# Heads' k, v and q products in pools of their own, gates through DRAM, two sets of projection banks, and first splits in another order

## The chip, the cores and the metric

The kernel runs on one core of a Trainium2 chip. The time is device microseconds of one execution. TensorE (PE) multiplies matrices into PSUM, VectorE (DVE) and ScalarE (ACT) work on tiles between PSUM and SBUF, GpSimd (POOL) helps them, and SyncE (SP) issues most of the DMAs. Each engine runs its own instructions in order, and waits on semaphores for those of the others.

## The reference, cut to what matters

Layer 0 is a gated pooling mixer, layer 1 a multi-head latent attention with 16 heads; SEQ is 512, D_MODEL 2048, W_A 4096, the latents have 512 channels.

```python
def pool_mixer_layer(x, norm_g, w_in, w_group, scale, w_out):
    h = rmsnorm(x, norm_g)
    proj = h @ w_in
    u, gate = proj[..., :W_A], proj[..., W_A:]
    pooled = jnp.stack([causal_mean_pool(u[:, :, gi], w) - u[:, :, gi] for gi, w in enumerate(POOL_WINDOWS)], axis=2)
    y = jnp.einsum('bsgc,gcd->bsgd', pooled, w_group).reshape(B, S, W_A) * scale
    y = y * jax.nn.silu(gate)
    return x + y @ w_out

def shared_kv(...):
    c = rmsnorm(c, kv_latent_g)
    kv = (c @ kv_w_b).reshape(B, S, N_HEADS, QK_NOPE + V_HEAD)
    k = qk_norm_rope(jnp.concatenate([k_nope, k_rope], axis=-1), k_norm_g, cos, sin)

def mla_layer(x, k, v, norm_g, w_in, q_latent_g, w_q_b, q_norm_g, w_out, cos, sin):
    proj = h @ w_in
    q_lat, gate = proj[..., :Q_LORA], proj[..., Q_LORA:]
    q = (rmsnorm(q_lat, q_latent_g) @ w_q_b).reshape(B, S, N_HEADS, QK_HEAD)
    q = qk_norm_rope(q, q_norm_g, cos, sin)
    o = chunk_causal_attention(q, k, v).reshape(B, S, W_B)
    return x + (o * jax.nn.silu(gate)) @ w_out
```

## The kernel before

Every product of float32 numbers is made of three matmuls: an operand is split into a high part, rounded by ACT (`A.copy`), and a low part, the rest, by DVE (`V.tensor_tensor(lo, src, f(hi), subtract)`; this helper, `split`, is at L147 to L149). PE then multiplies high by high, high by low and low by high. `load_w` (L115 to L127) fetches a tile of weights, raw, and splits it into `whi` (L125, ACT) and `wlo` (L126, DVE); `proj` with `mm3` (L143 to L145) multiplies it into one of three `mm` banks.

**Stage 1** is the first product, h @ w_in. Four output tiles are made by plain products (L357 to L382, 8 rounds of j): in each round two x tiles are loaded (`x_load`, L272 and L273), four weight tiles (L366), x is split with its gain (`gsplit`, L152 to L154), the weights are split in two halves of two tiles each, and PE runs L379 to L381. Round 0 is issued with high priority. The remaining 60 tiles are made in 30 pairs with seven products instead of eight (`w_combos`, `seven` with L328, L330, L332, and `gather`, L334 to L351, which puts the results together in a tile `e` and stores it in DRAM as `scr`). A pair takes four PSUM banks, k0 to k3, from a pool `ps7` with two buffers of each.

**Stage 2** takes the 4 groups of 8 tiles: `pooled_tile` (L428 on) loads a tile from `scr`, pools it and splits it into two `at` tiles; the eight of group 0 need no pooling any more and are issued with high priority. `y_tile` (L438 on) multiplies them by w_group (awg) and the gate; w_out (awo) follows. During group 0 the 16 x tiles are loaded again (xT, L458). The banks of stage 2 (`ps`: mm, sc, tr, ov) take the place of `ps7`.

**Attention.** `gate_unit` (L577 on) makes the 16 gates, silu of a projection, and keeps them in `at` tiles. Eight head groups of two heads follow. For the next group `prep_units` makes k and v (`kv_unit`, L613 to L615), q (`q_unit`, L633 to L635), the rotation of q on POOL (`qrot_unit`, L681 to L684) and the transposes (`tr_unit`; its u == 5 splits the rotary part of q in two halves, L714 on ACT and L715 on DVE). Beside it runs the attention of the present group: `score_unit` (scores L739, maximum L742, exp L747, scaling L748 and L749), two steps later `pt_unit` (transposes L758, split) and after each second one `pv_unit` (probabilities times v, L783 to L785; after the second of a head the product with the gate, L788). Two lists, one of attention and one of the preparation, are merged by due times (`LEAD`, `PACE`), and the tile framework's scheduler then sets each engine's order by the data and by when the pools' buffers come free. Last, `og_unit` splits the gated outputs and `out_unit` multiplies them by w_out (bwo); the first of these run beside the last group.

Pools: `xpool` (tiles `xt`, 16 buffers) holds raw k and q, v of group 0 and the split probabilities; `bpool` (`bt`, 32) holds transposed k and q and the later groups' v; `apool` (`at`, 32) holds latents and gates; the pool of `tt_` (7 in attention) holds probabilities, the rotary parts and other short-lived tiles. `tr` has two banks.

## Time and profile before

| | us |
|---|---|
| three runs | 1950.3, 1948.01, 1948.62 |
| profiled execution, its own time | 1948.62 |
| its span in the profile | 1946.8 |
| PE busy | 1920.0 (99%) |
| DVE, ACT, POOL busy | 1277.0, 822.7, 258.7 |
| DMA | 235.53 MB, mean 121 GB/s |

The busy time of PE counts a matmul from its start to its modelled end, so that neighbours overlap; how fast PE goes is read from start to start. In rows of single instructions the columns are the start, the duration, the engine and line, the operation and the tiles, and in square brackets how long the engine was idle before it and what released it. In tables by stretch each engine has its busy time and, in brackets, its instructions; then come the granted clock of TensorE, the DMA share and GB/s.

### The profile page before, as it was taken

The page shows a single profiled execution, that of the slowest core. Times are in us where ns is not written, and L with a number is a line of the kernel's source. Part 1 is how long each engine was busy: PE and PEld are TensorE (multiplying, and loading weights), DVE is VectorE, ACT ScalarE, POOL GpSimd, SP SyncE. Part 2 cuts the span into 40 slices and gives each one's busy share as a digit, 9 for nine tenths or more (in the row PEclk, how much of TensorE's full clock was granted, in tenths as well). Part 3 has the DMA queues.
Part 4 walks back from the last instruction along what each step waited for, and adds up shares of the span by engine and source line. Part 5 has one row for each costly group of instructions (what it writes and reads, how often), then busy time and mean ns, then how long its engine had stood idle before and what let it go on. Part 6 is the DMA issues. An engine that isn't in the chain of part 4 may idle for free.

```text
span 1946.8 us, 30577 instructions
## 1 busy us (share of the span) xinstructions
PE 1920.0 (99%) x11356; PEld 1707.5 (88%) x11356; DVE 1277.0 (66%) x2297; ACT 822.7 (42%) x1570; POOL 258.7 (13%) x405
## 2 busy tenths in 40 slices
PE   8999999999999999999999999999999999999999
PEld 7999999999999878888888888888888888888887
DVE  8677786896666687485685567473344888796432
ACT  7443433333333433333333454232244777785221
POOL 0433333344223000000000000000010111110000
PEclk9999999999999999999999999999999999999999
DMA  6545444445444655344334343333332111121632
GB/s 194 161 151 161 152 131 130 127 130 168 132 130 136 195 163 156 114 125 141 115 127 139 114 146 122 90 93 101 97 92 72 56 39 54 47 69 50 216 119 87
DMA packets 167894, 235.53 MB, mean 121 GB/s; under 512 B 14656, under 2 KB 94912, under 8 KB 167744
## 3 DMA queue, kind: packets, MB, share of 16 engines
q1 hardware_dynamic: 167568, 233.37, 38.4%
q8 instruction: 89, 1.46, 0.3%
q14 instruction: 61, 0.50, 0.1%
q10 hardware_dynamic: 144, 0.20, 0.0%
q0 software_dynamic: 32, 0.00, 0.0%
HBM read 208.35 MB, written 25.17 MB: 120 GB/s over the span
## 4 chain that ended last, share of the span: by engine, by line
PE 87%; DVE 5%; DMA 4%; ACT 3%; issue 1%; SPq 0%; POOL 0%; DVEq 0%; ACTq 0%; POOLq 0%
PE mm L145 14%; PE mm L143 14%; PE mm L144 14%; PE k L332 10%; PE k L328 9%; PE k L330 9%; PE sc L739 2%; PE mm L613 2%; PE mm L614 1%; PE mm L615 1%; PE mm L633 1%; PE mm L634 1%; PE k L379 1%; PE mm L635 1%; PE k L380 1%
## 5 line engine op out<-in xcount | busy, mean ns | idle before, releaser
L125 ACT CAST whi<-raw 128x512 fp32r<-128x512 f32 (+2 forms) x421 | 252.9, 608 | 515.6 <-PE mm L144 443.8
L328 PE MATMUL k<-xc,hi 128*128 128x256 f32 x1680 | 460.2, 283 | 0.0
L330 PE MATMUL k<-xc,hi 128*128 128x256 f32 x1680 | 460.2, 283 | 0.0
L126 DVE TENSOR_TENSOR wlo<-raw,whi 128x512 fp32r<-128x512 f32 (+2 forms) x421 | 281.1, 671 | 238.2 <-ACT whi L125 234.5
L332 PE MATMUL k<-xc,lo 128*128 128x256 f32 x1680 | 418.0, 284 | 0.4 <-DVE lo L312 0.2
L311 ACT CAST hi<-raw 128x1792 fp32r<-128x1792 f32 x120 | 202.8, 1690 | 359.6 <-PE k L332 240.6
L312 DVE TENSOR_TENSOR lo<-raw,hi 128x1792 fp32r<-128x1792 f32 x120 | 248.9, 2074 | 153.2 <-ACT hi L311 153.1
L145 PE MATMUL mm<-bt,wlo 128*128 128x512 f32 x860 | 336.0, 391 | 0.6 <-DVE wlo L126 0.6
L143 PE MATMUL mm<-bt,whi 128*128 128x512 f32 x860 | 335.1, 390 | 1.1 <-ACT bt L148 1.1
L144 PE MATMUL mm<-bt,whi 128*128 128x512 f32 x860 | 334.6, 389 | 0.0
L330 PEld LDWEIGHTS k<-xc,hi 128*128 128x128 f32 x1680 | 322.7, 192 | 0.0
L328 PEld LDWEIGHTS k<-xc,hi 128*128 128x128 f32 x1680 | 322.7, 192 | 0.0
L332 PEld LDWEIGHTS k<-xc,lo 128*128 128x128 f32 x1680 | 296.9, 192 | 1.5 <-DVE lo L312 1.0
L143 PE MATMUL mm<-at,whi 128*128 128x512 f32 x516 | 201.0, 391 | 1.9 <-DVE e L339 1.3
L144 PE MATMUL mm<-at,whi 128*128 128x512 f32 x516 | 201.9, 391 | 0.4 <-DVE at L149 0.4
L145 PE MATMUL mm<-at,wlo 128*128 128x512 f32 x516 | 201.4, 390 | 0.9 <-DVE wlo L126 0.9
L145 PEld LDWEIGHTS mm<-bt,wlo 128*128 128x128 f32 x860 | 161.5, 188 | 35.9 <-DVE wlo L126 2.2
L143 PEld LDWEIGHTS mm<-bt,whi 128*128 128x128 f32 x860 | 161.5, 188 | 35.3 <-ACT bt L148 1.6
L144 PEld LDWEIGHTS mm<-bt,whi 128*128 128x128 f32 x860 | 161.5, 188 | 33.6 <-DVE bt L149 0.2
L307 POOL TENSOR_TENSOR raw<-raw 128x256 f32<-128x256 f32 x120 | 99.9, 833 | 429.8 <-DVE raw L305 405.9
L143 PEld LDWEIGHTS mm<-at,whi 128*128 128x128 f32 x516 | 96.7, 188 | 22.6 <-DVE e L339 1.5
L145 PEld LDWEIGHTS mm<-at,wlo 128*128 128x128 f32 x516 | 96.9, 188 | 22.3 <-DVE wlo L126 2.3
(1150 smaller groups left out, 2589.1 us busy)
## 6 DMA issues: line engine op xcount, KB each, us to landing
raw<-awin SPq DMA_DIRECT2D x240, 256.0 KB, 3.3
raw<-awo SPq DMA_DIRECT2D x128, 256.0 KB, 2.8
raw<-bwin SPq DMA_DIRECT2D x80, 256.0 KB, 2.7
raw<-awg SPq DMA_DIRECT2D x64, 256.0 KB, 2.8
raw<-bwo SPq DMA_DIRECT2D x59, 256.0 KB, 2.8
scr<-e SPq DMA_DIRECT2D x56, 256.0 KB, 2.6
raw<-wkvb SPq DMA_DIRECT2D x32, 256.0 KB, 2.9
raw<-wqb SPq DMA_DIRECT2D x32, 192.0 KB, 2.4
```

Of the source, the lines that this page charges most:

```text
L125: A.copy(hi[:, :n], raw[:, :n])
L126: V.tensor_tensor(lo[:, :n], raw[:, :n], f(hi[:, :n]), ALU.subtract)
L143: T.matmul(dst, wh, xh, start=first, stop=False)
L144: T.matmul(dst, wh, xl, start=False, stop=False)
L145: T.matmul(dst, wl, xh, start=False, stop=last)
L307: G.tensor_tensor(c[:, :, 6, :], c[:, :, 4, :], c[:, :, 2, :], ALU.add)
L311: A.copy(hi, c[:, :, 1:8, :])
L312: V.tensor_tensor(lo, c[:, :, 1:8, :], f(hi), ALU.subtract)
L328: T.matmul(dst, hi[:, j % 2, wi, :], xh[j][:, xi, :], start=first, stop=False, skip_group_check=True)
L330: T.matmul(dst, hi[:, j % 2, wi, :], xl[j][:, xi, :], start=False, stop=False, skip_group_check=True)
L332: T.matmul(dst, lo[:, j % 2, wi, :], xh[j][:, xi, :], start=False, stop=last, skip_group_check=True)
L613: T.matmul(acc, ch[:, tsl], hi, start=(k == 0), stop=False)
```

## The change

Five things change. (1) In round j of the plain products the second x tile and the second half of the weights are loaded later, and the first half of the weights is split before the second x part; the rounds' x pools stand in another order; the load of `post` moves from POOL's queue to ACT's. (2) `ps7` becomes two pools with one buffer of each bank; the plain products take the second set, and pair n the set n % 2. (3) The first `y_tile` is issued only after the fourth split of group 0's pooled tiles. (4) Gates are stored in DRAM (`gd`), fetched into a `bt` tile at the third score of their head, multiplied there, and, but for the last head group, the gated output is stored in the same place and fetched again by `og_unit` into a `tt_` tile. (5) Raw k and v move to `at`, raw q to a new pool `qpool` of 5 buffers, for which `xpool` shrinks from 16 to 11; k's rotary part goes to `bt` from group 1 on.

```diff
@@ -77,8 +77,11 @@
-    def at(dt=F32R):
-        return apool.tile([P, S], dt, tag="a", name="at")
+    def qt(shape=(P, S)):
+        return qpool.tile(list(shape), F32, tag="q", name="qt")
+
+    def at(dt=F32R, shape=(P, S)):
+        return apool.tile(list(shape), dt, tag="a", name="at")
@@ -145,8 +148,7 @@
     def split(src, hi, lo):
-        A.copy(hi, src)
-        V.tensor_tensor(lo, src, f(hi), ALU.subtract)
+        return A.copy(hi, src), V.tensor_tensor(lo, src, f(hi), ALU.subtract)
@@ -174,7 +176,7 @@
     post = const.tile([P, 4], I32, name="post")
-    nc.gpsimd.dma_start(post, pos)
+    nc.scalar.dma_start(post, pos)
     tabs = {}
@@ -261,20 +263,22 @@
-        xcp = {j: c1.enter_context(tc.tile_pool(name=f"xcp{j}", bufs=1, **tile_)) for j in (3, 2, 6, 5, 4, 1, 0, 7)}
+        xcp = {j: c1.enter_context(tc.tile_pool(name=f"xcp{j}", bufs=1, **tile_)) for j in (4, 2, 6, 5, 3, 1, 0, 7)}
         w7 = c1.enter_context(tc.tile_pool(name="w7", bufs=2, **tile_))
-        ps7 = c1.enter_context(tc.tile_pool(name="ps7", bufs=2, space=bass.MemoryType.PSUM))
+
+        ps7 = [c1.enter_context(tc.tile_pool(name=f"ps7{i}", bufs=1, space=bass.MemoryType.PSUM, **tile_))
+               for i in range(2)]
         xh, xl = [None] * NJ, [None] * NJ
...
             nc.sync.dma_start(c[:, 2:8:5, :], xT[2 * j].rearrange("p (h t) -> p h t", h=2))
+            return c
+
+        def x_parts(j, c, hp):
+
             nc.sync.dma_start(c[:, 0:2, :], xT[2 * j + 1].rearrange("p (h t) -> p h t", h=2))
-            return c
-
-        def x_parts(j, c, hp):
-
             hl = xcp[j].tile([P, 2, 7, H], F32R, tag="xc", name="xc")
@@ -312,8 +316,8 @@
-        def banks():
-            return [ps7.tile([P, 2, H], F32, tag=f"k{i}", name=f"k{i}") for i in range(4)]
+        def banks(n):
+            return [ps7[n % 2].tile([P, 2, H], F32, tag=f"k{i}", name=f"k{i}") for i in range(4)]
@@ -351,7 +355,7 @@
-        accs = [ps7.tile([P, 2, H], F32, tag=f"k{i}", name=f"k{i}") for i in range(4)]
+        accs = banks(1)
         with ExitStack() as c2:
@@ -362,12 +366,14 @@
                 lo = w7.tile([P, 4, 2, P], F32R, tag="lo", name="lo")
-                for o in range(4):
-                    nc.sync.dma_start(
-                        raw[:, o, :, :], awin[32 + o][:, 2 * j * P:2 * (j + 1) * P].rearrange("p (k n) -> p k n", k=2))
-                h12, l12 = x_parts(j, c, hp)
-                for o in (0, 2):
-                    split(raw[:, o:o + 2], hi[:, o:o + 2], lo[:, o:o + 2])
+                parts = None
+                for m in (0, 2):
+                    for o in (m, m + 1):
+                        nc.sync.dma_start(raw[:, o, :, :], awin[32 + o][:, 2 * j * P:2 * (j + 1) * P].rearrange(
+                            "p (k n) -> p k n", k=2))
+                    parts = parts or x_parts(j, c, hp)
+                    split(raw[:, m:m + 2], hi[:, m:m + 2], lo[:, m:m + 2])
+                h12, l12 = parts
                 c4.close()
@@ -403,7 +409,7 @@
         for n, pair in enumerate((*range(18, 32), *range(16))):
-            ks = banks()
+            ks = banks(n)
             for q in range(NJ // 2):
@@ -412,14 +418,15 @@
                 V.tensor_tensor(sq[0], sq[0], sq[1], ALU.add)
-                p = ps7.tile([P, 2, H], F32, tag="k3", name="k3").rearrange("p h t -> p (h t)")
+                p = ps7[0].tile([P, 2, H], F32, tag="k3", name="k3").rearrange("p h t -> p (h t)")
                 ra[0] = norm_r(sq[0], D, p)
...
     bpool = ctx.enter_context(tc.tile_pool(name="bpool", bufs=32, **tile_))
-    xpool = ctx.enter_context(tc.tile_pool(name="xpool", bufs=16, **tile_))
+    xpool = ctx.enter_context(tc.tile_pool(name="xpool", bufs=11, **tile_))
+    qpool = ctx.enter_context(tc.tile_pool(name="qpool", bufs=5, **tile_))
     tp[0] = ca.enter_context(tc.tile_pool(name="tpool2", bufs=6, **tile_))
@@ -432,7 +439,7 @@
         hi, lo = at(), at()
-        split(x, hi, lo)
+        splits.append(split(x, hi, lo))
         return hi, lo
@@ -447,14 +454,22 @@
+    splits = []
     with tc.high_priority():
...
     for g in range(NG):
-        ys = [y_tile(g, o, pooled) for o in range(8)]
+        ys = []
+        for o in range(8):
+            with ExitStack() as c5:
+                if g == 0 and o == 0:
+
+                    for ins in splits[3]:
+                        c5.enter_context(tc.issue_after(ins.ins))
+                ys.append(y_tile(g, o, pooled))
         if g == 0:
...
             for k in range(KD):
-                x = xt()
+                x = xt() if k < 11 else qt()
                 nc.sync.dma_start(x, xT[k])
@@ -578,15 +593,17 @@
         V.tensor_tensor(z, acc, rb[0], ALU.mult)
-        sg = at(F32)
-        A.activation(sg, z, AF.Silu)
-        gates.append(sg)
+        A.activation(z, z, AF.Silu)
+        gd = dpool.tile([P, S], F32, tag="gd", name="gd")
+        nc.sync.dma_start(gd, z)
+        gates.append(gd)
...
     SC = 192.0 ** -0.5
-    st = {}
+    st, gated = {}, {}
+    nhg = NH // 2
@@ -594,11 +611,12 @@
         d["kvw"] = [load_w(wkvb[hg, :, k * 512:(k + 1) * 512], 512) for k in range(4)]
-        d["kraw"] = [xt((P, 2, 256)) for _ in range(2)]
+
+
+        d["kraw"] = [at(F32, (P, 2, 256)) for _ in range(2)]
         d["qraw"] = [None] * 4
-        vt = bt if hg else xt
-        d["vh"] = [vt((P, 2, 256), F32R) for _ in range(2)]
-        d["vl"] = [vt((P, 2, 256), F32R) for _ in range(2)]
+        d["vh"] = [at(F32R, (P, 2, 256)) for _ in range(2)]
+        d["vl"] = [at(F32R, (P, 2, 256)) for _ in range(2)]
         d["ssk"] = small(8, "ssk", 2)
@@ -633,7 +651,7 @@
             T.matmul(acc[:, 0:384], qh[:, tsl], lo[:, 0:384], start=False, stop=(k == 3))
-        q = xt((P, 2, 192))
+        q = qt((P, 2, 192))
         d["qraw"][t] = q
@@ -694,7 +712,11 @@
                     T.transpose(p[:, t * P:(t + 1) * P], d["krs"][h][:, t * P:(t + 1) * P], ident)
-                kh, kl = (xt(dt=F32R) if h else rpool.tile([P, S], F32R, tag="r", name="kr0")), bt()
+                if hg:
+                    kh = bt()
+                else:
+                    kh = xt(dt=F32R) if h else rpool.tile([P, S], F32R, tag="r", name="kr0")
+                kl = bt()
                 split(p, kh, kl)
@@ -715,8 +737,8 @@
             return
-        ft = xt if hg == 0 and u in (0, 3) else bt
-        hi, lo = ft(dt=F32R), ft(dt=F32R)
+        ft = at if hg == 0 and u in (0, 3) else bt
+        hi, lo = ft(), ft()
         if u in (3, 4):
@@ -727,6 +749,10 @@
         n = (i + 1) * P
+        if i == 2:
+
+            gt = d[("G", h)] = bt(dt=F32)
+            nc.sync.dma_start(gt, gates[2 * hg + h])
         s = sc()
@@ -784,8 +810,12 @@
         if pr == 1:
-            gt = gates[2 * hg + h]
+            gt = d.pop(("G", h))
             V.tensor_tensor(gt, ov, gt, ALU.mult)
+            if hg == nhg - 1:
+                gated[2 * hg + h] = gt
+            else:
+                nc.sync.dma_start(gates[2 * hg + h], gt)
@@ -818,9 +848,14 @@
     def og_unit(h):
-        nt = at if h < 14 else bt
+        nt = at if h < 8 else bt
         hi, lo = nt(), nt()
-        split(gates[h], hi, lo)
+        if h < 14:
+            x = tt_()
+            nc.sync.dma_start(x, gates[h])
+        else:
+            x = gated[h]
+        split(x, hi, lo)
         ogs[h] = (hi, lo)
@@ -840,7 +875,6 @@
-    nhg = NH // 2
     for o in range(12):
```

The shapes and the number of matmuls are the same. Three places show how instructions move. A row has a line, an operation, the tile written and, behind the arrow, those read, then the shape.

SP's first DMAs, before; xT is x, awin the weights of the plain products:

```order
L272 DMA raw<-xT 128x2x256
L273 DMA raw<-xT 128x512
L366 DMA hraw<-awin 128x256 x4
L272 DMA raw<-xT 128x2x256
L273 DMA raw<-xT 128x512
L366 DMA hraw<-awin 128x256 x4
```

and now:

```order
L276 DMA raw<-xT 128x2x256
L372 DMA hraw<-awin 128x256 x2
L281 DMA raw<-xT 128x512
L372 DMA hraw<-awin 128x256 x2
L276 DMA raw<-xT 128x2x256
L372 DMA hraw<-awin 128x256 x2
```

Two weight tiles have moved ahead of the second x tile. ACT's order goes with it; the first cast of weights (L151, which was L148) now stands ahead of the 512-wide x (L155, which was L153). Before:

```order
L153 ACTIVATE xc<-raw,cs 128x256
L153 ACTIVATE h_122<-raw,cs 128x256
L153 ACTIVATE xc<-raw,cs 128x512
L148 CAST hi<-hraw 128x512
L291 ACTIVATE raw<-raw,cs 128x2x256
```

and now:

```order
L155 ACTIVATE xc<-raw,cs 128x256
L155 ACTIVATE h_123<-raw,cs 128x256
L151 CAST hi<-hraw 128x512
L295 ACTIVATE raw<-raw,cs 128x2x256
L155 ACTIVATE xc<-raw,cs 128x512
```

The second place is DVE at the end of stage 1: the low halves of the last pair's weights (lo), of group 0's first weights (wlo) and of its pooled tiles (at), and the last pair's e. Before:

```order
L312 TENSOR_TENSOR lo_7395<-raw_7388,hi_7394 128x1792
L126 TENSOR_TENSOR wlo_7535<-raw_7533,whi_7534 128x512
L126 TENSOR_TENSOR wlo_7553<-raw_7551,whi_7552 128x512
L126 TENSOR_TENSOR wlo_7581<-raw_7579,whi_7580 128x512
L126 TENSOR_TENSOR wlo_7599<-raw_7597,whi_7598 128x512
L149 TENSOR_TENSOR at_7483<-tt__7480,at_7482 128x512
L149 TENSOR_TENSOR at_7489<-tt__7486,at_7488 128x512
L149 TENSOR_TENSOR at_7495<-tt__7492,at_7494 128x512
L149 TENSOR_TENSOR at_7501<-tt__7498,at_7500 128x512
L339 TENSOR_TENSOR e_7440<-e_7440,k0_7228 128x512
```

and now:

```order
L316 TENSOR_TENSOR lo_7398<-raw_7391,hi_7397 128x1792
L151 TENSOR_TENSOR at_7490<-tt__7487,at_7489 128x512
L151 TENSOR_TENSOR at_7496<-tt__7493,at_7495 128x512
L151 TENSOR_TENSOR at_7502<-tt__7499,at_7501 128x512
L151 TENSOR_TENSOR at_7508<-tt__7505,at_7507 128x512
L129 TENSOR_TENSOR wlo_7542<-raw_7540,whi_7541 128x512
L129 TENSOR_TENSOR wlo_7560<-raw_7558,whi_7559 128x512
L129 TENSOR_TENSOR wlo_7588<-raw_7586,whi_7587 128x512
L343 TENSOR_TENSOR e_7443<-e_7443,k0_7231 128x512
```

The four splits of pooled tiles have moved ahead of the weights'. On PE the first matmul of stage 2 waited for DVE's e (L339) and now waits for ACT's cast of its operands.

The third place is DVE in a head group in the middle, where the rotary half of the next q (L715, now L737) and the product with the gate (L788, now L814) stand. Before:

```order
L740 MEMSET sc_17027 64x64
L149 TENSOR_TENSOR xt_16669<-tr_16714,xt_16667 128x2x128
L740 MEMSET sc_17065 64x64
L715 TENSOR_TENSOR bt_16729<-tr_16723,bt_16729 64x512
L742 TENSOR_REDUCE nm_17034<-sc_17027 128x1
L149 TENSOR_TENSOR bt_16775<-mm_16794,bt_16773 128x256
L742 TENSOR_REDUCE nm_17072<-sc_17065 128x1
L149 TENSOR_TENSOR bt_16775<-mm_16820,bt_16773 128x256
L788 TENSOR_TENSOR at_13498<-ov_16608,at_13498 128x512
```

and now:

```order
L766 MEMSET sc_17690 64x64
L770 SCALAR_TENSOR_TENSOR nm_17659<-nm_17659,qy_17321 128x1
L768 TENSOR_REDUCE nm_17697<-sc_17690 128x1
L666 TENSOR_SCALAR sv_18121<-ssk_17977,kr2_12522 128x2
L814 TENSOR_TENSOR bt_17136<-ov_17229,bt_17136 128x512
L770 SCALAR_TENSOR_TENSOR nm_17697<-nm_17697,qy_17321 128x1
L737 TENSOR_TENSOR bt_17350<-tr_17344,bt_17350 64x512
L666 TENSOR_SCALAR sv_18121<-ssk_17977,kr2_12522 128x2
L151 TENSOR_TENSOR xt_17441<-tr_17438,xt_17440 128x128
L151 TENSOR_TENSOR xt_17441<-tr_17499,xt_17440 128x2x128
```

The product with the gate has moved ahead of the rotary half, and the splits of v (bt from mm) that stood between them are gone from here. The next transpose of probabilities on PE (L758, now L784) takes the bank that the rotary half empties, before and now.

2 lines of the change are left out of this document (1 added, 1 removed).

## The prediction

> **What bounds the kernel now.** I read the busy shares first, then the chain that ended last, then the busy time by stretch, then TensorE's waits, and only then single rows.
>
> ```profile
> PE 1920.0 (99%) x11356; PEld 1707.5 (88%) x11356; DVE 1277.0 (66%) x2297; ACT 822.7 (42%) x1570; POOL 258.7 (13%) x405
> PE 87%; DVE 5%; DMA 4%; ACT 3%; issue 1%; SPq 0%; POOL 0%; DVEq 0%; ACTq 0%; POOLq 0%
> ```
>
> TensorE (PE) is busy for 1920.0 of 1946.8 us and makes 87% of the chain. The change leaves the matmuls and their shapes as they are, so it can win only from TensorE's idle time, some 27 us, and where that lies decides everything.
>
> ```profile
> 0.00:50.00 50.00, 42.59 (x261) 38.68 (x262) 42.02 (x76) 39.59 (x67) 2.50 (x7) 1.00 0.63 194
> 600.00:650.00 50.00, 50.00 (x419) 50.00 (x418) 33.01 (x32) 17.70 (x13) 14.78 (x20) 1.00 0.39 122
> 650.00:700.00 50.00, 47.71 (x250) 39.92 (x250) 32.25 (x61) 23.59 (x39) 0.11 (x1) 1.00 0.74 242
> 1495.00:1536.00 41.00, 37.62 (x209) 31.95 (x209) 31.23 (x115) 30.41 (x99) 5.98 (x16) 1.00 0.15 46
> 1536.00:1575.00 39.00, 38.03 (x228) 33.64 (x227) 32.28 (x114) 28.78 (x99) 5.96 (x16) 1.00 0.16 49
> 1613.00:1651.00 38.00, 37.02 (x222) 32.64 (x221) 31.12 (x112) 28.35 (x97) 6.02 (x16) 1.00 0.16 50
> 1727.00:1765.00 38.00, 36.01 (x205) 31.70 (x204) 34.36 (x107) 29.27 (x85) 6.84 (x16) 1.00 0.25 75
> 1900.00:1947.00 47.00, 42.95 (x190) 35.24 (x188) 11.54 (x18) 7.48 (x12) 0.00 (x0) 1.00 0.27 85
> ```
>
> The columns are length, busy PE, weight loads, DVE, ACT and POOL, granted clock, DMA share and GB/s. Idle PE is 7.41 us at the start, 2.29 at the turn from the projections to the group matmuls (650 to 700), 3.38 and 0.97 in the first two stretches of attention, about 0.98 in each steady one, 1.99 in the last of them, and 4.05 after the last matmul, which the change doesn't touch.
>
> **The start.** The change puts two weight loads, their split and twelve narrow matmuls ahead of the second x load.
>
> ```profile
> 4.51 0.49 ACT L153 ACTIVATE h<-raw,cs 128x256 fp32r<-128x256 f32 x1
> 6.04 0.72 ACT L153 ACTIVATE xc<-raw,cs 128x512 fp32r<-128x512 f32 x1 [1.04 <-DMA raw<-xT]
> 6.74 0.62 ACT L148 CAST hi<-hraw 128x512 fp32r<-128x512 f32 x1
> 7.41 0.58 PE L379 MATMUL k<-xc,hi 128*128 128x256 f32 x1 [7.41 <-ACT hi L148]
> 7.79 0.41 PE L380 MATMUL k<-xc,hi 128*128 128x256 f32 x1
> ```
>
> The first matmul waits for the cast at 6.74, and this stands behind the 512-wide x at 6.04, which waited for the second x load. In the new order the cast follows row 4.51, so ACT is free at 5.00 and only the two weight loads (128 KB each, together as large as the x load) are awaited. If they land where the second x load did, the cast starts at 6.04 and PE at 6.04 + 0.67 = 6.7; if right when ACT is free, at 5.7. I take 6.3, a gain of 1.1. Behind it, what must be ready is the first pair's low half:
>
> ```profile
> 20.00:25.00 5.00, 5.00 (x34) 4.47 (x32) 4.96 (x9) 4.64 (x9) 0.00 (x0) 1.00 0.72 229
> 52.07 2.56 DVE L312 TENSOR_TENSOR lo<-raw,hi 128x1792 fp32r<-128x1792 f32 x1
> 55.25 0.52 PE L332 MATMUL k<-xc,lo 128*128 128x256 f32 x3
> ```
>
> DVE is full here (4.96 of 5), ends that row at 54.63, and PE wants it at 55.25: 0.62 of room. DVE itself can come earlier by anything from nothing to the whole 1.1; at 0.4 some **-1.0** is kept; bounds -0.3 (the weights land late, and DVE not earlier) and -1.6. The post load moved from POOL to ACT's queue is one small DMA behind the first constants, done before row 4.51's x is there: 0.
>
> [...] Rows 7.41 and 7.79 stand 0.38 apart, and a later 128x256 pair 0.12 apart, though the granted clock reads 1.00: the first matmuls are slow. [...]
>
> **Banks in two sets.** Stretch 600 to 650 has PE at 50.00 of 50: between the thirty pairs nothing waits for a bank, and two sets change nothing there: 0. At the turn it is otherwise.
>
> ```profile
> 660.98 0.28 PE L332 MATMUL k<-xc,lo 128*128 128x256 f32 x1
> 662.56 0.50 PE L143 MATMUL mm<-at,whi 128*128 128x512 f32 x1 [1.30 <-DVE e L339]
> 662.90 0.40 PE L144 MATMUL mm<-at,whi 128*128 128x512 f32 x1
> 663.13 0.39 PE L145 MATMUL mm<-at,wlo 128*128 128x512 f32 x1
> 667.45 0.39 PE L143 MATMUL mm<-at,whi 128*128 128x512 f32 x1
> 668.27 0.50 PE L144 MATMUL mm<-at,whi 128*128 128x512 f32 x1 [0.43 <-DVE at L149]
> 668.61 0.40 PE L145 MATMUL mm<-at,wlo 128*128 128x512 f32 x1
> 669.56 0.47 PE L143 MATMUL mm<-at,whi 128*128 128x512 f32 x1 [0.56 <-DVE e L342]
> ```
>
> Usual spacing is 0.12 for the pair matmuls and 0.23 for these (662.90 to 663.13), so three waits cost 1.46, 0.59 and 0.72, together 2.8. Two are for banks that the last pair's e must first empty; with the other set free they go. The middle one is for the last split of its eight, whose reload waited for the ring behind the splits that now come four places earlier; it goes too. What is late next is the weights:
>
> ```profile
> 684.00:688.00 4.00, 4.00 (x19) 3.23 (x18) 1.96 (x3) 1.26 (x2) 0.00 (x0) 1.00 1.05 390
> 669.44 1.17 SPq L351 DMA_DIRECT2D scr<-e  x2
> 670.71 4.43 SPq L458 DMA_DIRECT2D xt<-xT  x8
> 688.52 0.39 PE L145 MATMUL mm<-at,wlo 128*128 128x512 f32 x1
> 688.90 0.50 PE L143 MATMUL mm<-at,whi 128*128 128x512 f32 x1
> ```
>
> Sixteen xT loads saturate the DMA (1.05) until 688, and the next group weights stand behind eight of them (nine in the new order); PE loses 0.15 to them at 688.52 already (0.38 to the next start, against 0.23). SP sends them once e is stored at 669.44, and e should be done earlier by one or two us, as DVE no longer holds it behind the same reloads. If nothing of that comes about, PE waits at 688 for all that it won; if all of it, -2.8 stays. I take half, **-1.4**; bounds 0 and -3.
>
> **Gates and gated outputs through DRAM.** This adds 60 DMAs of 256 KB (15.7 MB). The nearest row is the e store:
>
> ```profile
> scr<-e SPq DMA_DIRECT2D x56, 256.0 KB, 2.6
> ```
>
> The DMA share is 0.15 to 0.25 in the attention stretches quoted; the gate is fetched two scores ahead of its product, several us, against 2.6 to land. It lies beside PE: 0. If SP sits behind a probability buffer for a gated load, that is a wait of up to 2.6 in the last group only; it is in the upper bound.
>
> **k, v and q in other pools.** With the fill no longer tied to the probabilities' ring, k, v and q matmuls are issued earlier. Before, each of six head groups has a stretch of 45 PE instructions with no fill, where PE waits on the DVE and ACT chain of softmax. After, I count one stretch of 42, four of 64, and one of about 127 in the sixth group. The price of a stretch stands in these rows:
>
> ```profile
> 1640.77 0.39 PE L739 MATMUL sc<-bt 128*128 128x512 f32 x1
> 1646.61 0.29 PE L758 MATMUL tr<-cs,tt__16648 128*128 128x128 f32 x1
> 1646.92 0.41 PE L758 MATMUL tr<-cs,tt__16693 128*128 128x128 f32 x2
> 1647.48 0.50 PE L613 MATMUL mm<-whi,at 128*128 128x512 f32 x1
> ```
>
> From the first to the last of them, seven gaps over 0.15 us above the usual spacing add up to 2.24 us. What replaces them:
>
> ```profile
> 1646.09 0.69 DVE L715 TENSOR_TENSOR bt<-tr,bt 64x512 fp32r<-64x512 f32 x1
> 1648.01 0.68 DVE L788 TENSOR_TENSOR at<-ov,at 128x512 f32<-128x512 f32 x1
> PE sc L739 <- ACT tt__14749 L747: 1.0, 1, 1.0
> PE tr L758 <- DVE nm L744: 0.9, 1, 0.9
> ```
>
> The transpose at 1646.92 needs the bank that the rotary half (L715, now L737) empties. Before, the gate product (L788, now L814) came after it; now it stands ahead, and must itself wait for the last pv matmul. Then PE waits for 0.69 + 0.69 and some 0.2 for starting, 1.5 to 1.6, where it waited 0.25. Three shorter waits of 0.3 to 0.35 go with it: 2.5 to 2.9 a group, +0.4 against 2.24, times four **+1.6**. The long stretch falls into the last of the quoted windows of attention, which idles 1.99 now; I put 3.3 there, **+1.3**, since many of its 127 instructions are wide scores that give the chain time. Against this stand the first two stretches of attention: of 3.38 and 0.97 the last two rows above (1.9) come before the changed order and stay; half of the remaining 2.45 goes with the fill, **-1.2**. PE also waits on 13 fewer semaphores (398 against 411 in the order), and a restart costs 0.11 (662.56 to 662.90, against 0.23): with some of them idle already, **-1.1**. Sum **+0.6**; bounds -6 (all stretches filled) and +7.
>
> **Sum.** -1.0 - 1.4 + 0.6 = -1.8. The profiled execution took 1948.62, which is also the median of the three runs, 1.8 above its span of 1946.8 for what lies around. So 1948.62 - 1.8 = **1946.8 us**. About 0.2%, or 3.9 us, is what can be told from no change: faster means under 1944.7, slower over 1952.5.
>
> **Rivals.**
> 1. *The new fill pays fully*: L737's wait is covered by a score that the sequencer already holds, the steady groups cost no more than before and the sixth group as much. Then +1.6 and +1.3 go, and the first stretches give their whole 2.45: 1946.8 - 2.9 - 1.2 = 1942.7. For it: DVE has 7 of 38 us idle in a steady stretch. Against: they are idle outside the dense part.
> 2. *Slower: the unfilled stretches price by their length.* At 2.24 us per 45 instructions, 64 cost 3.2 (+0.95, four times, 3.8) and 127 cost 6.3 (+4.1 over one of 45): +7.9 in place of +2.9, so 1951.8; and with the start and the turn at their upper bounds (-0.3 and 0) 1953.9. It decides from about 2.9 us a steady group on. For it: DVE and ACT are near full in such a stretch; against: part of the added instructions are wide scores, which give time.
> 3. *The turn keeps all*: -2.8 in place of -1.4, and the start -1.6: 1944.8, and with a third of rival 1 about 1943.5.
> 4. *The change does nothing at the turn or the start* (weights bound both): 1948.62 - 0.3 + 0.6 = 1948.9.
>
> **How the numbers follow.** Forecast 0.40, rival 1 0.22, rival 2 0.16, rival 3 0.10, rival 4 0.12. Rivals 1 and 3 are faster by over 0.2% for the most part, and the forecast's lower edge too: faster 0.40. Within: most of the forecast and rival 4, and rival 2 where only part of it comes: 0.43. Slower: the rest of rival 2 and the sixth group at its worst: 0.17. The range goes from 1938.5 (rivals 1 and 3 together, with filled stretches) to 1953.5 (rival 2 and its upper end).
>
> **What will show it.** Start: first matmul near 6.3, and the pair after the head without a wait for L316's low half. Turn: no wait for e; a wait for whi or wlo near 686 to 690 as long as what was won. DRAM: no PE wait whose releaser is a gate load. Attention: in the steady groups a PE transpose (L784) waiting 1.3 or more for L737; in the sixth group over 3 us of idle PE. I am wrong if the fill lands elsewhere in time than the order suggests, if exps wait on POOL's rotary products long enough to hold the scores, or if xT loads start late.

## The result, and the profile after

The kernel after takes 1968.35 us (median of 5 runs, 1966.04 to 1970.29); the kernel before, beside it on the same chip, 1950.1 (1948.01 to 1950.97). The ratio is 1.0095, with a 95% interval from 1.0083 to 1.0106: slower by 18 us, where 1946.8 was forecast. The profiled execution took 1966.04 with a span of 1964.3; it is 17.4 longer than the profiled execution of before.

The page of the kernel after, busy shares and shares of the chain that ended last:

```profile
PE 1925.4 (98%) x11356; PEld 1717.0 (87%) x11356; DVE 1272.7 (65%) x2297; ACT 822.6 (42%) x1570; POOL 256.3 (13%) x404
PE 84%; DVE 5%; ACT 4%; DMA 3%; issue 2%; SPq 1%; POOL 0%; DVEq 0%; ACTq 0%; POOLq 0%
```

PE does the same 11356 matmuls in 5.4 us more of busy time: some of them run slower. The busy time by stretch of the kernel after, in the stretches shown of before (length, PE, weight loads, DVE, ACT, POOL, granted clock, DMA share, GB/s):

```profile
0.00:50.00 50.00, 43.64 (x268) 39.77 (x269) 42.30 (x76) 39.22 (x66) 2.86 (x6) 1.00 0.60 183
50.00:100.00 50.00, 48.94 (x398) 48.14 (x397) 31.47 (x28) 21.25 (x20) 20.65 (x20) 1.00 0.52 169
650.00:700.00 50.00, 46.92 (x250) 38.82 (x249) 32.06 (x59) 22.85 (x39) 0.03 (x1) 1.00 0.73 242
1495.00:1536.00 41.00, 39.07 (x222) 35.31 (x221) 30.58 (x120) 30.18 (x104) 6.11 (x16) 1.00 0.27 82
1536.00:1575.00 39.00, 38.69 (x238) 35.59 (x238) 31.81 (x120) 30.43 (x104) 5.83 (x16) 1.00 0.22 70
1613.00:1651.00 38.00, 34.58 (x200) 31.11 (x199) 27.61 (x100) 26.77 (x91) 5.63 (x16) 0.96 0.25 77
1727.00:1765.00 38.00, 32.18 (x189) 29.43 (x189) 30.18 (x112) 24.52 (x76) 5.74 (x16) 0.82 0.25 80
```

The stretch 50 to 100 of before, for comparison:

```profile
50.00:100.00 50.00, 50.00 (x410) 49.57 (x409) 33.84 (x28) 21.48 (x21) 22.97 (x21) 1.00 0.50 159
```

Idle PE falls from 7.41 to 6.36 at the start and from 3.38 to 1.93 in the first stretch of attention. But 50 to 100, where before had PE at 50.00 of 50, now idles 1.06, the steady stretch 3.42 (0.98 before), and the last one 5.82 (1.99). And the granted clock, 1.00 in every stretch of before, is 0.96 and 0.82 in these two.

The waits of PE in the kernel after (us in total, times, longest):

```profile
PE tr L784 <- DVE bt L737: 7.4, 4, 1.8
PE mm L631 <- ACT qt L656: 4.9, 4, 1.3
PE tr L784 <- DVE bt L744: 3.5, 1, 3.5
PE k L336 <- DVE lo L316: 2.3, 4, 1.0
```

**A steady group.** The head groups are numbered hg 0 to 7; the four steady ones are hg 1 to 4, and the sixth group is hg 5. Rows of PE and of DVE in the kernel after, in the second steady group (hg 2):

```profile
1628.74 0.30 PE L784 MATMUL tr<-cs,tt__16113 128*128 128x128 f32 x1
1630.88 0.41 PE L784 MATMUL tr<-cs,tt__16158 128*128 128x128 f32 x2 [1.84 <-DVE bt L737]
1632.21 1.97 PE L765 MATMUL sc<-bt 128*128 128x384 f32 x5
```

```profile
1629.12 0.68 DVE L814 TENSOR_TENSOR bt<-ov,bt 128x512 f32<-128x512 f32 x1
1630.04 0.69 DVE L737 TENSOR_TENSOR bt<-tr,bt 64x512 fp32r<-64x512 f32 x1
```

The gate product (L814) does stand ahead of the rotary half (L737), and the transpose waits 1.84 for it. Behind that wait the scores run slowly: five of 128x384 take 1.97. The stretches around it show why (columns as above):

```profile
1628.83:1632.24 3.41, 1.32 (x9) 0.73 (x8) 3.01 (x9) 2.25 (x10) 3.12 (x11) 1.00 0.47 132
1632.24:1635.65 3.41, 3.41 (x14) 3.41 (x15) 2.19 (x9) 1.05 (x4) 0.80 (x2) 0.50 0.07 25
1738.05:1741.46 3.41, 1.53 (x14) 1.32 (x12) 2.32 (x5) 3.41 (x10) 0.00 (x0) 1.00 0.45 123
1741.46:1755.12 13.66, 10.26 (x40) 8.88 (x40) 10.12 (x37) 8.45 (x32) 5.74 (x16) 0.50 0.32 104
```

After 3.41 us with PE busy for 1.32 the granted clock is 0.50 for the next 3.41 us. This comes in the four groups hg 1 to 4, at 1591.3, 1632.2, 1673.2 and 1714.2, 40.96 us apart, and in the sixth group for 13.66 us on end. By an estimate, a full 3.41 us at half clock loses 1.7, and the 10.26 busy us of the sixth group at most 5.1: together at most 12 of the 17.4 us. The estimate is on the high side, since it takes all busy time as work that was slowed, and the busy time of PE grows by only 5.4; experiment 3 measures the four steady groups.

Where the difference lies, by the spacing of matmul starts (each gap less the median gap of its width, summed; idle time and slow clock are both in it; the first two lines by the times of matching matmuls; where the borders between the parts are drawn moves single lines by about 1 us):

| part | forecast | measured |
|---|---|---|
| start, up to the first group matmul (662.56, now 662.47) | -1.0 | -0.1 |
| turn up to attention (1491.2, now 1492.6) | -1.4 | +1.5 |
| first two stretches of attention (7.2, now 2.4) | -1.2 | -4.8 |
| four steady groups (12.3, now 23.0) | +1.6 | +10.7 |
| sixth group (3.0, now 12.2) | +1.3 | +9.2 |
| rest | -1.1 | +0.9 |

### The profile page after: what moved, and what is told of

Its sections match the earlier page's. It is cut to its first block, busy times and chain, and to the rows that moved or that the text cites. A ratio compares the mean times of both kernels' runs of the same rounds, so it can differ in the third digit from the quotient of the medians.

```text
span 1964.3 us, 30684 instructions
## 1 busy us (share of the span) xinstructions
PE 1925.4 (98%) x11356; PEld 1717.0 (87%) x11356; DVE 1272.7 (65%) x2297; ACT 822.6 (42%) x1570; POOL 256.3 (13%) x404
## 4 chain that ended last, share of the span: by engine, by line
PE 84%; DVE 5%; ACT 4%; DMA 3%; issue 2%; SPq 1%; POOL 0%; DVEq 0%; ACTq 0%; POOLq 0%
PE mm L146 15%; PE mm L148 15%; PE mm L147 15%; PE k L336 9%; PE k L334 9%; PE k L332 9%; PE sc L765 2%; PE mm L631 1%; PE mm L632 1%; PE mm L633 1%; DVE lo L316 1%; DMA raw<-awin 1%; PE tr L784 1%; DMA raw<-awg 1%; ACT whi L128 1%
## 5 line engine op out<-in xcount | busy, mean ns | idle before, releaser
L146 PE MATMUL mm<-bt,whi 128*128 128x512 f32 x944 | 367.2, 390 | 1.2 <-ACT bt L151 1.1
L148 PE MATMUL mm<-bt,wlo 128*128 128x512 f32 x944 | 368.4, 390 | 0.0
L147 PE MATMUL mm<-bt,whi 128*128 128x512 f32 x944 | 367.3, 389 | 0.0
L316 DVE TENSOR_TENSOR lo<-raw,hi 128x1792 fp32r<-128x1792 f32 x120 | 247.1, 2059 | 155.1 <-ACT hi L315 154.9
L146 PEld LDWEIGHTS mm<-bt,whi 128*128 128x128 f32 x944 | 177.1, 188 | 38.9 <-ACT bt L151 1.6
L148 PEld LDWEIGHTS mm<-bt,wlo 128*128 128x128 f32 x944 | 177.2, 188 | 37.6 <-DVE wlo L129 0.8
L147 PEld LDWEIGHTS mm<-bt,whi 128*128 128x128 f32 x944 | 177.2, 188 | 36.9 <-DVE bt L151 0.2
L146 PE MATMUL mm<-at,whi 128*128 128x512 f32 x432 | 167.7, 391 | 2.9 <-ACT whi L128 2.3
L147 PE MATMUL mm<-at,whi 128*128 128x512 f32 x432 | 169.2, 392 | 0.2 <-DVE at L151 0.2
L148 PE MATMUL mm<-at,wlo 128*128 128x512 f32 x432 | 168.2, 390 | 0.6 <-DVE wlo L129 0.6
L311 POOL TENSOR_TENSOR raw<-raw 128x256 f32<-128x256 f32 x120 | 101.9, 849 | 432.7 <-DVE raw L309 399.2
L312 POOL TENSOR_TENSOR raw<-raw 128x256 f32<-128x256 f32 x120 | 103.9, 866 | 9.2
L146 PEld LDWEIGHTS mm<-at,whi 128*128 128x128 f32 x432 | 80.8, 188 | 20.7 <-ACT whi L128 3.1
```

Source lines behind the costliest of these rows:

```text
L146: T.matmul(dst, wh, xh, start=first, stop=False)
L147: T.matmul(dst, wh, xl, start=False, stop=False)
L148: T.matmul(dst, wl, xh, start=False, stop=last)
L311: G.tensor_tensor(c[:, :, 6, :], c[:, :, 4, :], c[:, :, 2, :], ALU.add)
L312: G.tensor_tensor(c[:, :, 7, :], c[:, :, 6, :], c[:, :, 3, :], ALU.add)
L316: V.tensor_tensor(lo, c[:, :, 1:8, :], f(hi), ALU.subtract)
```

## The experiments

Each was timed in rounds beside the kernel before on its chip, and the ratio is to that; 1.0095 is the ratio of the kernel after. Lines named in the text are those of the kernel after unless said otherwise; where an edit adds or removes lines, the numbers in its rows shift by a few.

**1. Which part of the change.** The kernel after with the attention's parts, (4) and (5), undone:

```diff
-        d["kraw"] = [at(F32, (P, 2, 256)) for _ in range(2)]
+        d["kraw"] = [xt((P, 2, 256)) for _ in range(2)]
...
-        q = qt((P, 2, 192))
+        q = xt((P, 2, 192))
...
-            gt = d.pop(("G", h))
+            gt = gates[2 * hg + h]
```

> Keeps the new start, the two bank sets and the held first y tile, and has gates, raw k, q, v and the pools of attention as before. Theory A (attention makes the whole loss, the other parts come out even): the trace of the changed kernel reaches its first matmul of the attention stage about 1.4 us later than before, so 1951 to 1952 against 1950 for before, no stretch at half clock. Theory B (start and banks cost too): over 1956.

Measured: 1951.85 against 1950.21, ratio 1.0010 [1.0000, 1.0019]. The loss is in (4) and (5). Start, bank sets and the later first product together gain nothing.

**2. DRAM alone.** The kernel before with only the gates and gated outputs through DRAM:

```diff
-        sg = at(F32)
-        A.activation(sg, z, AF.Silu)
-        gates.append(sg)
+        A.activation(z, z, AF.Silu)
+        gd = dpool.tile([P, S], F32, tag="gd", name="gd")
+        nc.sync.dma_start(gd, z)
+        gates.append(gd)
```

> The kernel before, with gates and gated outputs through DRAM as its only change; pools of k, q and v as before. Theory A (transfers hidden): within 4 us of before, 1946 to 1954, no PE wait released by a gate load, and clock 1.00 throughout. Theory B (the transfers or the reload in the last group cost): 1955 or more, with the loss behind 1750 us.

Measured: 1952.05 against 1950.21, ratio 1.0007 [0.9998, 1.0017]. No wait of PE is released by a gate load: the 60 transfers are hidden to within some 3 us, and the loss is in the pools and in what they do to the order. The full clock that was expected throughout did not come. The profiled execution has two half-clock stretches of 3.41 us: one at 459.7, behind a wait of 2.17 for a pair's low half (L312) in stage 1, which this edit doesn't touch, and one at 1750.0, behind a wait of 1.92 for DVE.

**3. The clock by itself.** Thirteen repeated transposes on PE, put into the wait of hg 1 to 4:

```diff
-        for j in range(i + 1):
+        for j in (*range(i + 1), *([0] * 13 if h == 1 and i == 0 and 1 <= hg <= 4 else ())):
```

> The changed kernel, where the single transpose ahead of the long wait in head groups 1 to 4 is issued 14 times over (13 more of 0.11 us, into the same bank, 1.4 us in a wait of 2.1). Theory A (the granted clock falls because TensorE did almost nothing in one window, and that costs by itself): the four stretches at half clock go, some 1.2 to 1.5 us each, 1962 to 1964 in spite of 52 transposes more; the wait for L737 is shorter by what was filled in, the stretch in the sixth group stays. Theory B (the waits alone cost, the clock is a by-product without price): 1968 or more.

Measured: 1962.18 against 1950.21, ratio 1.0064 [1.0049, 1.0079], 6.2 us less than the kernel after. The same stretch in this run:

```profile
1628.83:1632.24 3.41, 3.11 (x26) 2.66 (x25) 3.23 (x12) 2.38 (x12) 0.63 (x3) 1.00 0.16 58
1632.24:1635.65 3.41, 3.25 (x21) 2.92 (x22) 2.89 (x11) 2.27 (x8) 3.40 (x10) 1.00 0.34 98
```

PE is given 52 matmuls more and the kernel gets faster: the four half-clock stretches are gone, and they cost 6.2 / 4 = 1.55 us a group. The wait itself is filled, not removed, and the q-copy waits (4.9 in 4) and the sixth group's 13.65 us at half clock are still there. This execution has another half-clock stretch at the turn, at 686.5, which that of the kernel after has not.

**4. The order on DVE.** The gate product put behind the rotary half in hg 1 to 4:

```diff
-            V.tensor_tensor(gt, ov, gt, ALU.mult)
+            with ExitStack() as c6:
+                if h == 0 and 1 <= hg <= 4:
+                    c6.enter_context(tc.issue_after(rot[-1].ins))
+                V.tensor_tensor(gt, ov, gt, ALU.mult)
```

> The changed kernel, with the product with the gate issued after the rotary half on DVE in head groups 1 to 4 (as it stood before). Theory A (this order lengthens one wait, and through it halves the clock): the wait of 1.84 us falls to about 1.0, the four stretches at half clock go, and the time falls by 4 times 0.8 + 1.4, so about 1959. Theory B (only the wait): 1965. Theory C (the longer unfilled stretch sets it, not this order): 1967 or more.

Measured: 1965.09, ratio 1.0081 [1.0066, 1.0096], theory B's number. The wait fell from 1.84 to at most 1.1, but three of four half-clock stretches stayed. Two stretches of this run, each with the one behind it:

```profile
1592.69:1596.10 3.41, 1.81 (x13) 1.41 (x13) 3.25 (x10) 2.60 (x11) 3.01 (x10) 1.00 0.16 60
1596.10:1599.51 3.41, 3.41 (x15) 3.22 (x15) 2.08 (x9) 1.55 (x6) 0.92 (x3) 0.50 0.29 94
1633.65:1637.06 3.41, 1.98 (x13) 1.77 (x14) 3.25 (x10) 2.60 (x12) 3.41 (x12) 1.00 0.30 88
1637.06:1640.48 3.42, 3.42 (x28) 3.15 (x27) 2.85 (x13) 2.37 (x9) 0.45 (x2) 1.00 0.19 66
```

With PE busy for 1.81 us of the stretch the clock halves, with 1.98 it stays here. A wait over a third shorter was worth little here, as the clock halved all the same.

**5 and 6. Which tiles.** Only raw q back to the probabilities' pool (16 buffers again), and only raw k and v as before:

```diff
-        q = qt((P, 2, 192))
+        q = xt((P, 2, 192))
```

> The changed kernel with raw q back among the xt tiles (16 buffers, no pool of its own); k, v, gates, start and banks stay changed. In the order the stretches without fill shrink: from 7.3 us of work to 3.3 to 4.2 in the middle groups, and from 15.1 to 9.0 in the last. Theory Q (q's own pool lets q's products run ahead, so that later nothing is left to fill): no half clock in the middle groups, no wait of 3.5 us for L744, 1946 to 1952. Theory K (k and v in the other pool do it): 1962 or more.

```diff
-        d["kraw"] = [at(F32, (P, 2, 256)) for _ in range(2)]
-        d["vh"] = [at(F32R, (P, 2, 256)) for _ in range(2)]
-        d["vl"] = [at(F32R, (P, 2, 256)) for _ in range(2)]
+        d["kraw"] = [xt((P, 2, 256)) for _ in range(2)]
+        vt = bt if hg else xt
+        d["vh"] = [vt((P, 2, 256), F32R) for _ in range(2)]
+        d["vl"] = [vt((P, 2, 256), F32R) for _ in range(2)]
```

> The changed kernel with raw k and v in the pools of before, and raw q in its own pool. In the order the stretches without fill are 7.4 to 7.5 us of work in six groups and 8.3 in the last. Theory Q: each such stretch costs what it costs in the changed kernel, 5 to 6 us with its half clock, against 3 before, so six times 2 to 3 more than before: 1962 to 1968. Theory K: 1948 to 1954, no half clock. In both the 13.7 us at half clock in the sixth group go, since its stretch of 15.1 is gone.

Measured: 1960.84, ratio 1.0047 [1.0032, 1.0062], with raw q back, and 1963.58, 1.0062 [1.0045, 1.0079], with raw k and v back. Raw q back takes half of the loss away and fell between both theories: the gate product again stands ahead of a rotary half, now of the other one, which scores wait for (4.1 us in 3 waits). Raw k and v back gave what the theory named for q said. With either change of pools left out, the order still has half-clock stretches in it: in the first two in the middle groups, at 1659.6 and 1700.6, and 6.8 and 3.4 us in the sixth; in the second two in the middle groups, at 1650.3 and 1691.3, two earlier ones, of 3.4 us at 1530.8 and 6.8 at 1571.8, and 6.8 us in the sixth.

**7. The start alone.** The kernel before with the loads and splits of (1) in the new order:

```diff
+                for m in (0, 2):
+                    for o in (m, m + 1):
+                        nc.sync.dma_start(raw[:, o, :, :], awin[32 + o]...
+                    parts = parts or x_parts(j, c, hp)
+                    split(raw[:, m:m + 2], hi[:, m:m + 2], lo[:, m:m + 2])
```

> The kernel before, with the new order of loads and splits in the plain products as its only change. Theory A (the start's gain is given back): the first matmul comes about 1 us earlier than 7.4, and PE then waits 1 to 2 us for L312's low half between 50 and 100 us; within 2 us of before. Theory B (it is kept, and the bank sets give it back): no such wait, 1 us faster at 164 us, 1949 against 1950.

Measured: 1950.47 against 1950.64, ratio 0.9998 [0.9989, 1.0008]. Its first stretches:

```profile
0.00:50.00 50.00, 43.30 (x269) 39.42 (x270) 42.31 (x76) 39.64 (x66) 3.56 (x7) 1.00 0.60 186
50.00:100.00 50.00, 48.40 (x395) 47.65 (x394) 32.31 (x26) 20.77 (x20) 20.75 (x20) 1.00 0.52 167
```

What is won before 50 us (idle 6.70 for 7.41) is idle again before 100 (1.60, where before had none): one wait of 1.5 us for the low half of a pair's weights stands there, and there are five such waits, 4.0 us together, in the whole execution.

**8. Both: raw q back and the rotary half first.** Experiment 5 with the order of 4, in hg 0 to 6.

```diff
-        q = qt((P, 2, 192))
+        q = xt((P, 2, 192))
...
+                if h == 0 and 0 <= hg <= 6:
+                    c6.enter_context(tc.issue_after(rot[-1].ins))
```

> The kernel with raw q back among the xt tiles (1960.8 before this edit), and the product with the gate issued after the rotary half on DVE in head groups 0 to 6. There a score waited 1.4 us for L736, which stood behind the product, which stood behind the last pv matmul. Theory A (this order on DVE makes the low window in every variant): that wait falls under 0.5 us, the half clock in the middle groups goes, 1954 to 1956. Theory B (the fill's place makes it): 1959 or more.

Measured: 1954.0 against 1951.0, ratio 1.0018 [1.0009, 1.0028]. The middle groups keep the full clock; one half-clock stretch of 6.8 us in the sixth group is left. Most of the 18 us is gone though k, v and the gates still go the new way. Raw q back alone gave about half (experiment 5); with it, DVE's order is worth another 6 to 7 us, where it was worth about 3 with q in its own pool (experiment 4). So neither of the two does it by itself.

**9. The clock in the sixth group.** Experiment 3, and the first two scores of the seventh group four times over:

```diff
-        for j, (l, r) in enumerate(ops):
+        for j, (l, r) in list(enumerate(ops)) * (4 if hg == 6 and h == 0 and i < 2 else 1):
```

> The changed kernel with 13 more transposes in head groups 1 to 4 (1962.2 so), and in addition the first two scores of the seventh group, which stand right at the wait of 3.5 us for L744, issued four times over (15 matmuls of 128 and 15 of 256 columns more, 2.7 us of work). Theory A (half clock costs by itself): the 13.7 us at half clock go or shrink to one window of 3.4, 1958 to 1960. Theory B (the wait and the chain behind it set that stretch): 1962 to 1964.

Measured: 1965.98 against 1951.0, ratio 1.0079 [1.0064, 1.0094], slower than both theories allowed. Most of the added scores fell behind the wait and ran at half clock themselves; the 13.65 us and the 3.5 us wait stayed. The run says nothing of the price of the sixth group's half clock.

**10. The order on ACT.** Why does PE wait for q copies? Rows of ACT and of PE in the kernel after, in hg 2, and then ACT in the sixth group:

```profile
1614.11 1.65 ACT L128 CAST whi<-raw 128x512 fp32r<-128x512 f32 x3
1615.92 1.28 ACT L678 ACTIVATE tt__16406<-krr,sy 128x128 f32<-128x128 f32 x4
1617.10 1.22 ACT L656 COPY qt<-mm 128x384 f32<-128x384 f32 x3
```

```profile
1615.80 0.48 PE L765 MATMUL sc<-bt 128*128 128x128 f32 x2
1617.62 0.51 PE L631 MATMUL mm<-whi,at 128*128 128x512 f32 x1 [1.33 <-ACT qt L656]
1743.05 1.11 PE L784 MATMUL tr<-cs,tt__17765 128*128 128x128 f32 x4 [3.47 <-DVE bt L744]
```

```profile
1737.40 1.65 ACT L128 CAST whi<-raw 128x512 fp32r<-128x512 f32 x3
1739.21 1.28 ACT L678 ACTIVATE tt__18140<-krr,sy 128x128 f32<-128x128 f32 x4
1740.39 1.23 ACT L656 COPY qt<-mm 128x384 f32<-128x384 f32 x3
1741.49 0.72 ACT L743 ACTIVATE bt<-tr,gqk 128x512 fp32r<-128x512 f32 x1
```

In both places ACT works without a break, but on weights, key scalings and q copies for later products, and what PE needs now (the q copy, and the q split L743 that L744 follows) comes last. In the sixth group the split is one of hg 6; the copies ahead of it are of hg 7, the last, and the weights are those of the output product, as hg 7's are all cast by then. So the key's scalings were moved behind the q copies:

```diff
-        for t in range(4):
-            for h in range(2):
-                c = 2 * t + h
-                A.activation(d["krs"][h]...
+        d["ky"] = y
...
         if u == 2:
+            d["kr"], y = [], d["ky"]
+            for t in range(4):
+                for h in range(2):
+                    c = 2 * t + h
+                    A.activation(d["krs"][h]...
```

> The kernel after, with the eight scalings of the key by its norm in every group after the first moved on ScalarE from ahead of the three raw q copies to behind the last of them; nothing else differs. Theory A (ScalarE's order makes the q waits): the four scalings that stood between the whi split and the q copies (1.28 us together in the trace of after) no longer delay the copies, so the wait of matmul L631 for the q copy falls from 1.2-1.3 us to under 0.4 in the four groups that have it, and the 3.5 us wait of the sixth group falls by 1 to 1.5; the time falls by 4 to 6 us to 1962-1964 us. Theory B (something else, such as the filling of the projection's bank, holds the copies back): the waits stay over 1 us and the time is 1967 us or more.

Measured: 1960.01 against 1949.76, ratio 1.0046 [1.0029, 1.0063]. Its waits (L785, L738 and L745 are L784, L737 and L744 of the kernel after):

```profile
PE tr L785 <- DVE bt L738: 4.0, 3, 1.4
PE tr L785 <- DVE bt L745: 2.4, 1, 2.4
PE mm L631 <- ACT qt L656: 1.8, 4, 1.2
```

The q waits fall from 4.9 to 1.8 (one of the four still takes 1.2) and the sixth group's by 1.1, as theory A has it for the most part. The time falls by more than it said, since three of the four middle half-clock stretches go as well. Why the wait for L738 shortens with it, from 7.4 to 4.0, was not looked into.

**11. Both orders.** Experiment 10 with the rotary half first in all groups but the last:

```diff
+                if h == 0 and hg < nhg - 1:
+                    c6.enter_context(tc.issue_after(rot[-1].ins))
```

> The same move of the key's scalings on ScalarE, and the product of gate and output put behind the rotary half on VectorE, in every group but the last. Theory A (the two orders together are the loss in the steady groups): both PE waits of a steady group, for the rotary half (1.84 us) and for the q copy (1.3 us), fall under 0.8 us, the half-clock stretches of 3.4 us in the middle groups go, and the time is 1954-1958 us; what is left above the kernel before is the sixth group. Theory B (moving one piece only puts another late): a new wait of over 1 us a group stands before PE, some half-clock stretches stay, and the time is 1962 us or more.

Measured: 1960.89, ratio 1.0059 [1.0044, 1.0074], between the theories and no better than 10. One middle stretch kept half clock, another got it, and the sixth group has 13.65 us of it again. The two orders don't add up.

**12. The sixth group.** Experiment 10, with the q copies of the last group (hg 7) behind the second q split of hg 6, which PE awaits in the sixth group's stretch:

```diff
+        with ExitStack() as c6:
+            if hg == 7:
+                c6.enter_context(tc.issue_after(st[6]["t4"].ins))
+            A.copy(q.rearrange("p h d -> p (h d)"), acc[:, 0:384])
```

> The kernel of the run with the key's scalings behind the q copies, and, in the sixth group alone, the four raw q copies of the last group put on ScalarE behind the scaled split of the present group's second q half (there they come one ahead of the first scaled split and three between the two). Theory A (in the sixth group too it is ScalarE's order, the next group's q copies and weight splits ahead of the present group's q split, that TensorE waits for): the wait of the transposes L784 for L744, 3.47 us in the kernel after and 2.36 us with the key's scalings moved, falls under 1.2 us, the half-clock stretch that follows it (3.4 us at 1735) goes and the second (6.8 us at 1742) may, and the time is 1954-1958 us. Theory B (the q copies only move the wait to the products that need the projection's banks, or the chain of softmax behind them is the bound): TensorE's idle time in the stretch 1734 to 1775 stays and the time is 1959 us or more.

Measured: 1957.72 against 1949.64, ratio 1.0049 [1.0031, 1.0066], within theory A's range. The stretch of the sixth group in the kernel before, in the kernel after, in experiment 10 and in this one:

```profile
1734.00:1775.00 41.00, 39.01 (x213) 33.17 (x213) 31.08 (x95) 26.75 (x75) 6.84 (x16) 1.00 0.21 62
```

```profile
1734.00:1775.00 41.00, 34.52 (x198) 30.18 (x197) 31.61 (x95) 26.90 (x77) 5.74 (x16) 0.83 0.28 85
```

```profile
1734.00:1775.00 41.00, 34.44 (x194) 29.87 (x194) 31.51 (x93) 27.05 (x75) 4.71 (x14) 0.88 0.36 110
```

```profile
1734.00:1775.00 41.00, 37.02 (x211) 31.10 (x210) 33.45 (x105) 26.90 (x75) 4.80 (x13) 0.96 0.44 137
```

The wait for the q split is gone and PE gets 2.6 us more done there than in 10; two half-clock stretches of 3.4 us stay, at 1730.1 and 1740.4, and one in the middle groups, at 1668.7. The profiled execution is 3.8 faster than that of 10, but the ratios to the kernel before don't tell the two apart. That ACT's order makes this wait is shown; that it makes the whole of the sixth group's loss is not.

No version beat the kernel before: experiments 1, 2 and 7 stand within 0.2% of it.

## Why the prediction was wrong, step by step

**The step that failed** is the price of the attention stretches, "2.5 to 2.9 a group, +0.4 against 2.24, times four +1.6" and "+1.3" for the sixth. The order on DVE was read rightly, and its wait nearly: 1.5 to 1.6 was worked out for the transpose behind the rotary half, and it waits 1.84. Measured are +10.7 for the four groups and +9.2 for the sixth. Three things were left out.

1. *A gap was priced at its length.* Every steady group loses another 1.55 at half clock behind the gap: experiment 3 gets 6.2 back from the four. The sixth loses at most 5.1 by the estimate from its rows, which no run shows. This is the largest part, up to 11 of the 17.4.
2. *The wait for the q copies*, 1.2 to 1.3 in each of four groups, was not seen. The working followed DVE's order alone, to the rotary half; on ACT the key scalings and weight splits moved ahead of the copies as well (experiment 10).
3. *The sixth group* was priced by what its wide scores give back. PE waits for ACT there instead: 1.65 + 1.28 + 1.23 of work for later products stand ahead of the split that PE waits 3.47 for. With ACT's order changed that wait goes (experiment 12); how much of the 9.2 it makes stays open. Over 3 us of idle PE had been named as the sign, and came.

For a steady group 0.4 + 1.55 + 1.3 = 3.25, against 10.7 / 4 = 2.7 measured: the terms are of the right size and don't simply add up.

**The first stretches** gained more than the 1.2 put down, 4.8 by the spacing of starts: PE gets 222 and 238 matmuls done there, where before it had 209 and 228. That the fill does this fits, but no run tries it alone. The **-1.1** for fewer waits on semaphores shows nowhere: the rest of the kernel is 0.9 longer.

**Start.** First matmul forecast near 6.3, measured 6.36:

```profile
4.61 0.49 ACT L155 ACTIVATE h<-raw,cs 128x256 fp32r<-128x256 f32 x1
5.69 0.62 ACT L151 CAST hi<-hraw 128x512 fp32r<-128x512 f32 x1 [0.59 <-DMA hraw<-awin]
6.36 0.58 PE L385 MATMUL k<-xc,hi 128*128 128x256 f32 x1 [6.36 <-ACT hi L151]
```

The 1.05 won there was to be kept, as DVE's full stretch would start 0.4 earlier. It is not: 50 to 100 idles 1.06 more, with two waits for L316's low half, 1.1 together, and experiment 7 shows it on its own. The -1.0 is -0.1 by the time of the first group matmul, beyond its bound of -0.3. The slow first matmuls are a small part of it: they last from 7.41 to 11.45 before and from 6.36 to 10.91 after, 0.5 us longer. Those of 128x256 start 0.21 apart there and 0.12 later, so by an estimate some 0.2 is lost.

**Turn.** The rows of PE in the kernel after:

```profile
662.47 0.40 PE L146 MATMUL mm<-at,whi 128*128 128x512 f32 x1
684.23 0.50 PE L146 MATMUL mm<-at,whi 128*128 128x512 f32 x1 [1.48 <-ACT whi L128]
688.33 0.50 PE L146 MATMUL mm<-at,whi 128*128 128x512 f32 x1 [0.80 <-ACT whi L128]
689.61 0.50 PE L148 MATMUL mm<-at,wlo 128*128 128x512 f32 x1 [0.55 <-DVE wlo L129]
```

The wait of 1.30 for e is gone, as forecast; the weights take it back with 1.48 + 0.80 + 0.55 = 2.83 of idle time, as much as the 2.8 that were to be won. So the bound of 0 that the working named held, not the half that it took, and the part up to attention is even 1.5 longer. Experiment 1, with both start and turn, puts the two together at 0.0 to 0.2% slower.

**DRAM** at 0 was right within what experiment 2 can tell, some 3 us.

**The rivals.** Rivals 1 and 3 were wrong: the steady groups cost 10.7 more, not less, and the turn kept nothing. Rival 4 was right for start and turn. Rival 2 had the right sign and place, at 1951.8 to 1953.9; its price by length missed the same clock as the forecast did.

## What to carry to other kernels

Freed buffers let a scheduler pull the next stage's work forward on every engine, and on engines that run in order it then stands ahead of what the matmuls need now (here PE waits 1.84 us behind the gate product on DVE and 1.33 behind key scalings and weights on ACT): read the new order on all of them, ACT's too, before taking a fill for a gain. Don't price a new wait by its length alone, but look at the granted clock behind it. Here a wait of 1.84 left PE busy for 1.32 of 3.41 us, the next 3.41 ran at half clock, and that cost another 1.55 a group (experiment 3); in the sixth group, where PE, waiting for ACT and DVE, was busy for 10.26 of 13.66 us behind it, half clock held for all of them. Work won at the very start is kept only if the engine that is late next, here DVE at the first pairs, comes earlier as well: in experiment 7 PE idles 0.71 less up to 50 us and 1.60 more from there to 100.

## What the runs showed of the hardware

The half-clock stretches of the kernel after (the one after the last matmul is left out here) begin at 1591.3, 1632.2, 1673.2, 1714.2 and 1741.5: 40.96 us apart three times, then 27.3, which are 12 and 8 times 3.4133. Four last 3.41 us, the fifth 13.65, four times as long. In the profiled executions before and after, cut up into stretches of 3.4133 from the end of the slow first matmuls (11.45 and 10.91) to 1940 us, five stretches at full clock are followed by half clock, and in these PE is busy for 1.32 to 1.53 us. All the others at full clock are followed by full clock, and in these PE is busy for 2.06 us or more. So PE need not be idle throughout. In the experiments it went both ways: 1.81 was followed by half clock twice (experiment 4), 1.93 once (experiment 10), 1.98 twice by full clock (experiments 4 and 10) and once by half (experiment 11, rows below). 1.68 in experiment 10 (684.16 to 687.57) was followed by full clock, 2.19 in experiment 5 (1697.16 to 1700.57) by half. The busy time alone gives no sharp limit.

```profile
1558.84:1562.25 3.41, 1.98 (x15) 1.54 (x14) 1.73 (x7) 3.41 (x11) 0.00 (x0) 1.00 0.00 0
1562.25:1565.66 3.41, 3.41 (x12) 2.92 (x12) 2.97 (x10) 1.70 (x8) 0.00 (x0) 0.50 0.00 0
```

A wait of 1.84 us, in a stretch with PE idle for 2.09 in all, was enough for half clock in the kernel after. The slow first matmuls end at 10.91 there, which is 463 times 3.4133 before the half clock at 1591.3; they end at 11.45 in the profiled execution before, and between 8.90 and 12.60 in the experiments' executions. So their place differs from one execution to the next. In experiment 4 the two executions with a mean granted clock of 0.993 took 1967.98 and 1966.44 us, the two with 0.995 and 0.996 1963.62 and 1963.73; that the place of the stretches makes this difference was not shown.

Not every half-clock stretch belongs to the change. In the profiled executions of experiments 2, 4, 5, 10, 11 and 12 one stands in stage 1, at 457 to 460, behind a single PE wait of 2.0 to 3.0 us for a pair's low half; in the profiled execution before that wait is 0.2. Experiment 7 has one at 1531.95, in an attention that is that of before. So a difference of some 4 us between two single executions is not yet one between two kernels.
